# Moving the loads of a rotary-embedding kernel from a casting GpSimd DMA queue to float32 loads on SyncE's hardware queue, with ScalarE doing the cast and smaller buffer pools

## Chip, cores, metric

One core of one Trainium2 chip. The metric is the time of one execution on the device, in microseconds. All runs quoted here are fast (a single core, granted clock 1.0). "Span" is what the profiler shows from the first to the last instruction; a measured time is about 2 us longer than the span of the same run. The experiments ran in three later sessions, on chips that the record numbers 5, 3 and 12; the kernel before was measured again in each (medians 322.81, 323.12 and 323.17 us), and the ratios are taken within a session. Where two changed kernels of different sessions are subtracted below, that shift of up to 0.5 us is in the difference.

## The reference

```python
x: (8, 2048, 16, 64) float32      cos, sin: (2048, 32) float32
x1, x2 = x[..., :32], x[..., 32:]
out1 = x1 * cos - x2 * sin        # cos, sin broadcast over batch and heads
out2 = x1 * sin + x2 * cos
return concatenate([out1, out2], -1)          # float32, same shape as x
```

x and the output are 67.1 MB each. The arithmetic is slight, so this kernel mostly moves data: 16 tiles, each with a 4 MiB float32 read and a 4 MiB float32 write in HBM.

## The kernel before

Everything that moves goes through GpSimd's DMA queue. A load casts float32 to float16 on the way in, and a store casts float16 to float32 on the way out. The code is shortened: views and broadcasts are left out, and `# ...` marks a cut.

```python
const_pool = tile_pool(name="rope_const", bufs=1)
io_pool  = tile_pool(name="rope_io", bufs=3)      # xt and ot, three of each
tmp_pool = tile_pool(name="rope_tmp", bufs=3)
# ... the tables, cast on the way in
nc.gpsimd.dma_start(out=cos_sb, in_=cos_src)
nc.gpsimd.dma_start(out=sin_sb, in_=sin_src)

for it in range(NT * B):                          # 16 tiles
    # ...
    xt = io_pool.tile([P, J, H, D], f16)
    nc.gpsimd.dma_start(out=xt, in_=x[...])       # float32 -> float16
    ot = io_pool.tile([P, J, H, D], f16)
    # ... v1, v2
    nc.vector.tensor_mul(out=ot, in0=xt, in1=cos)  # 128x8192
    nc.vector.tensor_mul(out=v1, in0=x2, in1=sin)  # 128x4096, as the next three
    nc.vector.tensor_mul(out=v2, in0=x1, in1=sin)
    nc.vector.tensor_sub(out=o1, in0=o1, in1=v1)
    nc.vector.tensor_add(out=o2, in0=o2, in1=v2)
    nc.gpsimd.dma_start(out=out[...], in_=ot)     # float16 -> float32
```

The scheduler orders GpSimd's queue as four loads, four stores, four loads, and so on. The queue is one line: a store that is issued behind a load runs after it (the packet times below show one that stood 13.6 us).

## Time and profile before

| | before |
|---|---|
| measured | 322.81 us (median of 3; 322.52 to 323.58) |
| span | 321.2 us |
| VectorE busy | 210.7 us, 66% |
| DMA busy | 9 tenths or more in 38 of 40 slices |
| HBM read + written | 134.7 MB, 419 GB/s over the span |

From the page of the kernel before: the span, and the rows that cut it into 40 equal slices (busy tenths; GB/s that the DMA engines moved), then the HBM total.

```profile
span 321.2 us, 191 instructions
...
DVE  0089999970009999994004999999100799999800
...
DMA  6999999999999999999999999999999999999994
GB/s 98 212 218 214 218 275 433 428 445 424 314 226 202 222 220 361 445 433 428 445 231 214 224 204 240 439 416 449 433 373 224 208 216 224 288 449 441 416 449 167
...
HBM read 67.63 MB, written 67.11 MB: 419 GB/s over the span
```

DMA is full from start to end, and VectorE (DVE) idles for whole slices. The GB/s row alternates between about 215 (loads) and about 435 (stores), and that is not a difference in speed. The profile counts the bytes that land, and a casting load lands half of what it reads, so loads read about 430 GB/s as well. One 4 MiB transfer of either kind takes 4.19 MB / 432 GB/s = 9.7 us, and 32 of them take 310 us.

The issues part of the same page (line, operation, count, KB each, median us from issue to landing):

```profile
out_dram<-ot POOLq DMA_DIRECT2D x16, 4096.0 KB, 20.4
xt<-in_x_dram POOLq DMA_DIRECT2D x16, 2048.0 KB, 24.5
cos_sb<-in_cos_dram POOLq DMA_DIRECT2D x1, 128.0 KB, 3.2
sin_sb<-in_sin_dram POOLq DMA_DIRECT2D x1, 128.0 KB, 3.3
```

The tables lead the queue and land 3.3 us after issue. The timeline of GpSimd's queue near the end (start us, us, instruction, idle before and who ended it):

```profile
260.39 0.54 POOL L44 DMA_DIRECT2D xt<-in_x_dram  x1 [32.02 <-DVE v L66]
264.79 0.54 POOL L72 DMA_DIRECT2D out_dram<-ot  x1 [3.87 <-DVE ot L70]
277.94 0.54 POOL L72 DMA_DIRECT2D out_dram<-ot  x1 [12.61 <-DVE ot L70]
291.08 0.53 POOL L72 DMA_DIRECT2D out_dram<-ot  x1 [12.61 <-DVE ot L70]
304.22 0.53 POOL L72 DMA_DIRECT2D out_dram<-ot  x1 [12.61 <-DVE ot L70]
```

VectorE makes a tile every 13.1 us, but a store takes only 9.7 us. In spite of that the DMA row stays at 9. The packet records say why: the last four stores began to move at 278.4, 288.2, 297.9 and 307.6 us. The first of them was issued at 264.79 and stood 13.6 us behind loads in the same queue. That backlog (stores issued that still wait for the DMA engines) shrinks by about 3.4 us per store (13.1 less 9.7) and lasts just to the end.

### The profile page before, as it was taken

The page shows a single profiled execution, that of the slowest core. Times are in us where ns is not written, and L with a number is a line of the kernel's source. Part 1 is how long each engine was busy: PE and PEld are TensorE (multiplying, and loading weights), DVE is VectorE, ACT ScalarE, POOL GpSimd, SP SyncE. Part 2 cuts the span into 40 slices and gives each one's busy share as a digit, 9 for nine tenths or more (in the row PEclk, how much of TensorE's full clock was granted, in tenths as well). Part 3 has the DMA queues.
Part 4 walks back from the last instruction along what each step waited for, and adds up shares of the span by engine and source line. Part 5 has one row for each costly group of instructions (what it writes and reads, how often), then busy time and mean ns, then how long its engine had stood idle before and what let it go on. Part 6 is the DMA issues. An engine that isn't in the chain of part 4 may idle for free.

```text
span 321.2 us, 191 instructions
## 1 busy us (share of the span) xinstructions
DVE 210.7 (66%) x80; POOL 18.9 (6%) x38
## 2 busy tenths in 40 slices
DVE  0089999970009999994004999999100799999800
POOL 4001000010000100002000000000200000000000
DMA  6999999999999999999999999999999999999994
GB/s 98 212 218 214 218 275 433 428 445 424 314 226 202 222 220 361 445 433 428 445 231 214 224 204 240 439 416 449 433 373 224 208 216 224 288 449 441 416 449 167
DMA packets 5153, 100.94 MB, mean 314 GB/s; under 512 B 544, under 2 KB 1056, under 8 KB 1056
## 3 DMA queue, kind: packets, MB, share of 16 engines
q0 software_dynamic: 5152, 100.93, 100.0%
q14 instruction: 1, 0.01, 0.0%
HBM read 67.63 MB, written 67.11 MB: 419 GB/s over the span
## 4 chain that ended last, share of the span: by engine, by line
DVE 46%; DMA 27%; issue 20%; POOL 2%; POOLq 0%; DVEq 0%; PEldq 0%
DMA xt<-in_x_dram 27%; DVE ot L59 16%; DVE v L66 8%; DVE v L65 8%; DVE ot L70 8%; DVE ot L69 5%; POOL out_dram L72 1%; POOL cos_sb L37 0%; POOL sin_sb L38 0%; POOLq L101 0%; POOL xt L44 0%; POOLq L72 0%; DVEq L59 0%; PEldq L101 0%; POOLq L44 0%
## 5 line engine op out<-in xcount | busy, mean ns | idle before, releaser
L59 DVE TENSOR_TENSOR ot<-xt,cos_sb 128x8192 f16<-128x8192 f16 x16 | 70.7, 4421 | 93.2 <-DMA xt<-in_x_dram 93.1
L70 DVE TENSOR_TENSOR ot<-ot,v 128x4096 f16<-128x4096 f16 x16 | 36.6, 2285 | 0.0
L65 DVE TENSOR_TENSOR v<-xt,sin_sb 128x4096 f16<-128x4096 f16 x16 | 36.6, 2285 | 0.0
L69 DVE TENSOR_TENSOR ot<-ot,v 128x4096 f16<-128x4096 f16 x16 | 36.6, 2285 | 0.0
L66 DVE TENSOR_TENSOR v<-xt,sin_sb 128x4096 f16<-128x4096 f16 x16 | 36.6, 2285 | 0.0
L72 POOL DMA_DIRECT2D out_dram<-ot x16 | 8.6, 535 | 166.9 <-DVE ot L70 166.9
L44 POOL DMA_DIRECT2D xt<-in_x_dram x16 | 8.6, 550 | 117.9 <-DVE v L66 117.9
L37 POOL DMA_DIRECT2D cos_sb<-in_cos_dram x1 | 0.8, 825 | 0.8 <-PEq L101 0.8
L38 POOL DMA_DIRECT2D sin_sb<-in_sin_dram x1 | 0.7, 733 | 0.0
L90 POOL MEMSET const-float32-0.0<- 128x1 f32 x1 | 0.1, 98 | 0.2 <-issue 0.2
L90 POOL MEMSET const-bfloat16-1.0<- 128x1 bf16 x1 | 0.1, 101 | 0.0
L90 POOL MEMSET const-float32-1.0<- 128x1 f32 x1 | 0.1, 98 | 0.0
L90 POOL MEMSET const-uint8-127<- 128x1 uint8 x1 | 0.1, 98 | 0.0
## 6 DMA issues: line engine op xcount, KB each, us to landing
out_dram<-ot POOLq DMA_DIRECT2D x16, 4096.0 KB, 20.4
xt<-in_x_dram POOLq DMA_DIRECT2D x16, 2048.0 KB, 24.5
cos_sb<-in_cos_dram POOLq DMA_DIRECT2D x1, 128.0 KB, 3.2
sin_sb<-in_sin_dram POOLq DMA_DIRECT2D x1, 128.0 KB, 3.3
```

The lines of the kernel that those rows point to most:

```text
L37: nc.gpsimd.dma_start(out=cos_sb, in_=cos_src)
L38: nc.gpsimd.dma_start(out=sin_sb, in_=sin_src)
L44: nc.gpsimd.dma_start(out=xt, in_=x[b, s0 : s0 + T2].rearrange("(p j) h d -> p (j h d)", j=J),)
L59: nc.vector.tensor_mul(out=ot.rearrange("p j h (e d) -> p j (h e) d", d=Dh), in0=xt.rearrange("p j h (e d) -> p j (h e) d", d=Dh), in1=cos ...
L65: nc.vector.tensor_mul(out=v1, in0=x2, in1=sin_bb)
L66: nc.vector.tensor_mul(out=v2, in0=x1, in1=sin_bb)
L69: nc.vector.tensor_sub(out=o1, in0=o1, in1=v1)
L70: nc.vector.tensor_add(out=o2, in0=o2, in1=v2)
L72: nc.gpsimd.dma_start(out=out[b, s0 : s0 + T2].rearrange("(p j) h d -> p (j h d)", j=J), in_=ot,)
L90: nc = _bacc.Bacc("TRN2", target_bir_lowering=False, num_devices=1)
```

## The change

The intent is to let loads run on a queue of their own, so that they no longer wait in GpSimd's order behind stores, and to spare GpSimd their issue. The load now lands as float32, and ScalarE, idle until now, casts in SBUF. A float32 load buffer is twice as large, and the other pools are cut: three load buffers, two float16 buffers, two output buffers (before: three), one set of temporaries (before: three).

```diff
-    io_pool = ctx.enter_context(tc.tile_pool(name="rope_io", bufs=3))
-    tmp_pool = ctx.enter_context(tc.tile_pool(name="rope_tmp", bufs=3))
+    in_pool = ctx.enter_context(tc.tile_pool(name="rope_in", bufs=3))
+    half_pool = ctx.enter_context(tc.tile_pool(name="rope_half", bufs=2))
+    out_pool = ctx.enter_context(tc.tile_pool(name="rope_out", bufs=2))
+    tmp_pool = ctx.enter_context(tc.tile_pool(name="rope_tmp", bufs=1))
 ... (cos and sin: still two casting loads on GpSimd's queue)
-        xt = io_pool.tile([P, J, H, D], f16)
-        nc.gpsimd.dma_start(
-            out=xt,
+        xf = in_pool.tile([P, J * H * D], f32)
+        nc.sync.dma_start(
+            out=xf,
             in_=x[b, s0 : s0 + T2].rearrange("(p j) h d -> p (j h d)", j=J),
         )
+        xt = half_pool.tile([P, J, H, D], f16)
+        nc.scalar.copy(out=xt.rearrange("p j h d -> p (j h d)"), in_=xf)
 
-        ot = io_pool.tile([P, J, H, D], f16)
+        ot = out_pool.tile([P, J, H, D], f16)
```

More of the change, by code (lines that the diff above doesn't have):

```diff
@@ L20 @@
     f16 = mybir.dt.float16
+    f32 = mybir.dt.float32
     B, S, H, D = x.shape
@@ L29 @@
     const_pool = ctx.enter_context(tc.tile_pool(name="rope_const", bufs=1))
-    io_pool = ctx.enter_context(tc.tile_pool(name="rope_io", bufs=3))
-    tmp_pool = ctx.enter_context(tc.tile_pool(name="rope_tmp", bufs=3))
-    cos_src = cos.rearrange("(t p j) d -> p t (j d)", p=P, j=J)
-    sin_src = sin.rearrange("(t p j) d -> p t (j d)", p=P, j=J)
+    in_pool = ctx.enter_context(tc.tile_pool(name="rope_in", bufs=3))
+    half_pool = ctx.enter_context(tc.tile_pool(name="rope_half", bufs=2))
+    out_pool = ctx.enter_context(tc.tile_pool(name="rope_out", bufs=2))
+    tmp_pool = ctx.enter_context(tc.tile_pool(name="rope_tmp", bufs=1))
     cos_sb = const_pool.tile([P, NT, J * Dh], f16)
     sin_sb = const_pool.tile([P, NT, J * Dh], f16)
-    nc.gpsimd.dma_start(out=cos_sb, in_=cos_src)
-    nc.gpsimd.dma_start(out=sin_sb, in_=sin_src)
+    nc.gpsimd.dma_start(out=cos_sb, in_=cos.rearrange("(t p j) d -> p t (j d)", p=P, j=J))
+    nc.gpsimd.dma_start(out=sin_sb, in_=sin.rearrange("(t p j) d -> p t (j d)", p=P, j=J))
     for it in range(NT * B):
```

## The prediction

> **What bounds the kernel now.** DMA. The row of forty slices shows the DMA engines at 9 in every slice but the first and last, while VectorE is 66% busy and idles for whole slices. HBM read plus written is 134.7 MB, 419 GB/s over the 321.2 us span. In slices that hold only stores the page shows 428 to 449 GB/s. In slices that hold only loads it shows 202 to 226, but it counts the float16 that lands; the float32 read is twice that, about 430. So a 4 MiB transfer, load or store, costs about 4.19 MB / 432 GB/s = 9.7 us, and the cast makes a load no cheaper. Thirty-two of them are 310 us; about 11 us is start and end. The Trainium skill ("DMA: Bandwidth & Descriptors", Where 436 GB/s comes from) names a ceiling of 435 GB/s; the trace agrees to within its slices. The long waits in the waits view (VectorE for xt, 93.1 us; the store issue for VectorE, 166.9 us) are slack: the single queue always has work behind them, down to the last store.
>
> **What the change removes.** The blocking of loads behind stores in GpSimd's program order (groups of four loads, then four stores; the load issue waited 117.9 us for VectorE), and the loads' GpSimd issue time, 16 x 0.55 us, off the path. SBUF traffic of a load doubles (4 MiB land instead of 2), HBM traffic stays. The same skill page (Issuing engines are not separate DMA queues) says that all queues run on the same 16 engines, so I expect no more bandwidth: loads again about 9.7 us alone, about 19.4 us while a store shares the engines.
>
> **What it adds.** Sixteen ScalarE copies of 128x8192. The skill ("ScalarE: Activation LUTs", What ACT_TABLE_LOAD costs) gives 186 ns + 0.833 ns per element: an estimate of 7.0 us each, 112 us in all, overlapped with DMA except at the start and end. VectorE work per tile stays 4.42 + 4 x 2.29 = 13.4 us of records (13.1 us apart), 210 us in all.
>
> **What reaches the critical path.** Start: the first load leaves on SyncE's own queue rather than after cos and sin, saving about 2 us; but cos and sin now share the engines with 4 MiB loads and may land late (estimate 9 to 45 us), delaying VectorE. Loads prefetch meanwhile, so DMA stays busy. Middle: VectorE needs 13.1 us per tile against 19.4 us of DMA, so DMA still sets the pace. End: before, all last loads were done at about 280 us and a backlog of stores kept DMA full. After, loads and stores share, so the last load lands near 275 to 295 us, followed by copy 7.0, VectorE 13.1, store issue latency about 2.5, store 9.7: about 32 us, in which DMA has only about two other stores (20 us), or VectorE's 13.1 us per tile paces the remaining stores of 9.7. I estimate 8 to 14 us of idle DMA there.
>
> Sum: 3 start + 310 + 11 idle + 1.6 end + 1.6 (measured time minus profiled span, from before) = about 327.5 us.
>
> **What would show it.** ScalarE copy near 7.0 us x16. Average DMA rate in the middle near 430 GB/s, with loads and stores mixed. DMA below 9 tenths in some of the last five slices. VectorE total unchanged near 211 us. SyncE load waits on ScalarE.
>
> **What would make it wrong.** Hardware-queue float32 loads slower than 430 GB/s (at 409 it is about 335 us); small load packets starved by store packets, or the reverse; late sin delaying VectorE enough to empty the DMA queue early; or a backlog of stores long enough to hide the end (about 318 us).
>
> I expect 327.5 us, range 319 to 337; faster by over 2% 0.05, within 2% 0.53, slower by over 2% 0.42.

## The result

The changed kernel took 331.82 us (median of 4; 331.79 to 331.92), beside 322.66 us for the kernel before in the same rounds (median of 4). The ratio is 1.028, with a 95% interval of 1.0264 to 1.0296: slower by 2.8%. A ratio here is the mean time of one kernel's fast runs over the mean of the other's fast runs of the same rounds, so it is not quite the ratio of the medians.

The page of the changed kernel, the same rows:

```profile
span 330.1 us, 233 instructions
...
DVE  0005059999194884929578392955929398999940
...
DMA  8999997989999999999999999999999999975967
GB/s 320 420 419 436 403 447 318 441 385 445 445 445 441 385 445 445 445 421 405 445 445 445 409 417 445 445 442 413 417 445 441 445 389 441 381 318 246 389 254 318
...
HBM read 67.63 MB, written 67.11 MB: 408 GB/s over the span
```

HBM traffic is the same to the digit. In the middle the DMA row is full. There are dents at about one sixth of the span and in the last five slices. The groups of instructions and the issues, same columns as before (a group's line: count, busy us, mean ns, idle before and its releaser):

```profile
L50 ACT CAST xt<-xf 128x8192 f16<-128x8192 f32 x16 | 112.3, 7018 | 179.1 <-DVE v L68 164.8
L61 DVE TENSOR_TENSOR ot<-xt,cos_sb 128x8192 f16<-128x8192 f16 x16 | 70.8, 4423 | 91.1 <-DMA out_dram<-ot 65.3
L67 DVE TENSOR_TENSOR v<-xt,sin_sb 128x4096 f16<-128x4096 f16 x16 | 36.5, 2283 | 14.4 <-DMA sin_sb<-in_sin_dram 14.4
...
xf<-in_x_dram SPq DMA_DIRECT2D x16, 4096.0 KB, 36.0
out_dram<-ot POOLq DMA_DIRECT2D x16, 4096.0 KB, 27.4
cos_sb<-in_cos_dram POOLq DMA_DIRECT2D x1, 128.0 KB, 24.5
sin_sb<-in_sin_dram POOLq DMA_DIRECT2D x1, 128.0 KB, 42.6
```

VectorE's new waits are for an output buffer that a store has not yet emptied (65.3 us in all), and once for sin (14.4 us). sin now lands 42.6 us after issue instead of 3.3.

The dents, looked at closely: stretches of time (us from the span's start), their length, busy us and instructions of each engine, PEclk (TensorE's granted clock, which nothing here uses), share of DMA busy, GB/s. The engines stand in the order VectorE, ScalarE, GpSimd.

```profile
53.30:55.30 2.00, 2.00 (x2) 2.00 (x1) 0.57 (x1) 1.00 0.61 262
109.00:245.00 136.00, 92.57 (x35) 49.13 (x7) 3.74 (x7) 1.00 1.08 432
...
289.20:292.30 3.10, 3.10 (x2) 3.10 (x1) 0.53 (x1) 1.00 0.40 169
292.40:302.20 9.80, 9.80 (x5) 1.02 (x1) 0.00 (x0) 1.00 0.89 374
302.30:305.50 3.20, 3.20 (x2) 0.00 (x0) 0.53 (x1) 1.00 0.38 164
305.60:315.30 9.70, 9.70 (x5) 0.00 (x0) 0.00 (x0) 1.00 0.90 378
315.40:318.70 3.30, 1.62 (x1) 0.00 (x0) 0.53 (x1) 1.00 0.37 159
```

This view spreads a transfer's bytes over neighbouring stretches, so it shows a dent rather than a zero. The packet records are sharper: no packet at all moves from 53.2 to 55.3, 289.1 to 292.4, 302.3 to 305.6 and 315.4 to 318.7 us. Those are one gap of 2.1 us and three of 3.3 us, 12.0 us in all. VectorE is busy in all of them except half of the last.

And GpSimd's queue near the end, in the changed kernel:

```profile
276.27 0.53 POOL L74 DMA_DIRECT2D out_dram<-ot  x1 [18.87 <-DVE ot L72]
291.02 0.53 POOL L74 DMA_DIRECT2D out_dram<-ot  x1 [14.22 <-DVE ot L72]
304.17 0.53 POOL L74 DMA_DIRECT2D out_dram<-ot  x1 [12.61 <-DVE ot L72]
317.31 0.53 POOL L74 DMA_DIRECT2D out_dram<-ot  x1 [12.61 <-DVE ot L72]
```

The last three stores are issued 13.1 us apart, as before. But now their packets begin 1.4 us after each issue (292.4, 305.6, 318.7): there is no backlog, and the DMA engines wait for VectorE after every store.

The account, by the packet records (fast profiled runs):

| us | before | after |
|---|---|---|
| first packet of the kernel | 3.7 | 2.0 |
| time in which any DMA engine moved data | 315.9 | 314.5 |
| gaps with no packet at all | 0.0 | 12.0 |
| last packet to end of span (taken equal, see below) | 1.6 | 1.6 |
| span | 321.2 | 330.1 |

Start and transfer work are each a little better, by 1.6 (unrounded) and 1.4 us, and the gaps cost 12.0. (The records have a clock of their own. It is tied to the span here by taking the end as 1.6 us after the last packet; in both kernels the first load's last packet then ends within 0.1 us of the instruction that waited for it. The second row counts a moment as busy when at least one of the 16 engines moves data, so engines that wait for one another do not show as gaps.)

### The profile page after: what moved, and what is told of

It reads as the page before. It is cut to its first block, busy times and chain, and to the rows that moved or that the text cites. A ratio compares the mean times of both kernels' runs of the same rounds, so it can differ in the third digit from the quotient of the medians.

```text
span 330.1 us, 233 instructions
## 1 busy us (share of the span) xinstructions
DVE 211.5 (64%) x80; ACT 113.6 (34%) x17; POOL 10.3 (3%) x22
## 4 chain that ended last, share of the span: by engine, by line
issue 59%; DMA 22%; DVE 13%; POOL 2%; POOLq 0%; PEldq 0%
DMA sin_sb<-in_sin_dram 13%; DMA out_dram<-ot 9%; DVE ot L61 4%; DVE ot L71 3%; DVE v L68 3%; DVE v L67 2%; DVE ot L72 2%; POOL out_dram L74 2%; POOL cos_sb L38 0%; POOLq L103 0%; POOLq L74 0%; PEldq L103 0%
## 5 line engine op out<-in xcount | busy, mean ns | idle before, releaser
L50 ACT CAST xt<-xf 128x8192 f16<-128x8192 f32 x16 | 112.3, 7018 | 179.1 <-DVE v L68 164.8
L61 DVE TENSOR_TENSOR ot<-xt,cos_sb 128x8192 f16<-128x8192 f16 x16 | 70.8, 4423 | 91.1 <-DMA out_dram<-ot 65.3
L67 DVE TENSOR_TENSOR v<-xt,sin_sb 128x4096 f16<-128x4096 f16 x16 | 36.5, 2283 | 14.4 <-DMA sin_sb<-in_sin_dram 14.4
L50 ACT ACT_TABLE_LOAD x1 | 1.3, 1283 | 0.7 <-PEq L92 0.7
## 6 DMA issues: line engine op xcount, KB each, us to landing
sin_sb<-in_sin_dram POOLq DMA_DIRECT2D x1, 128.0 KB, 42.6
```

The lines of the kernel that those rows point to most:

```text
L50: nc.scalar.copy(out=xt.rearrange("p j h d -> p (j h d)"), in_=xf)
L61: nc.vector.tensor_mul(out=ot.rearrange("p j h (e d) -> p j (h e) d", d=Dh), in0=xt.rearrange("p j h (e d) -> p j (h e) d", d=Dh), in1=cos ...
L67: nc.vector.tensor_mul(out=v1, in0=x2, in1=sin_bb)
```

## The experiments

Theory A: the DMA engines do the same work at the same rate. The loss is their idle time: at the end, where VectorE paces the last stores and there is no backlog, and early, where the tables are late. That the small output pool decides the backlog was not yet part of it: for the second run A expected that a third output buffer would not help. This came with theory A1, after that run missed. Rival B: float32 loads on the hardware queue, landing twice the bytes and hopping through ScalarE, cost more per tile. Every run was correct except one. In the notes below, "n load / m output" counts float32 load buffers and output buffers; the changed kernel has 3 / 2.

### Tables ahead of x on SyncE's queue (3 / 2)

```diff
-    nc.gpsimd.dma_start(out=cos_sb, in_=cos...)
-    nc.gpsimd.dma_start(out=sin_sb, in_=sin...)
+    cos_f = const_pool.tile([P, NT, J * Dh], f32)
+    sin_f = const_pool.tile([P, NT, J * Dh], f32)
+    nc.sync.dma_start(out=cos_f, in_=cos...)
+    nc.sync.dma_start(out=sin_f, in_=sin...)
+    nc.scalar.copy(out=cos_sb, in_=cos_f)
+    nc.scalar.copy(out=sin_sb, in_=sin_f)
```

> As after, but cos and sin come in float32 on SyncE's queue ahead of the first x load and ScalarE casts them. Theory A (same DMA work; the added time is 12.0 us of idle DMA: 2.1 us early because sin lands at 44.7 us, and 3 x 3.3 us in the tail where VectorE paces the last stores): sin is there before 10 us, the early gap goes, the lead of loads over stores shrinks by about two tiles so one of the three tail gaps goes too; estimate 325.6 us (324 to 327.5). Rival B (a float32 load on the hardware queue, with its doubled landing and its ScalarE hop, costs about 0.55 us more per tile throughout): only the first microseconds change, 329 to 332 us.

Measured: 328.65 us, ratio to before 1.019 (1.017 to 1.021). The early gap and one of the three tail gaps went, as A said; two of 3.3 us stayed. But it missed A's 325.6 by 3 us and lies between the two forecasts, so by itself it settles little. Two things were not in the estimate. The first copy of x began at 16.9 us instead of 13.2. And the 16 DMA engines ran up to 5.4 us apart: the completion records of one load in mid kernel began between 143.1 and 148.5 us, against 0.2 us apart in the changed kernel. The time in which any DMA engine moved data rose from 314.5 to 316.7 us, so "the same work" of A does not hold here. Why the engines drifted, and whether the drift is what made it longer, is open.

### Two load buffers, three output buffers (2 / 3)

```diff
-    in_pool = ctx.enter_context(tc.tile_pool(name="rope_in", bufs=3))
+    in_pool = ctx.enter_context(tc.tile_pool(name="rope_in", bufs=2))
-    out_pool = ctx.enter_context(tc.tile_pool(name="rope_out", bufs=2))
+    out_pool = ctx.enter_context(tc.tile_pool(name="rope_out", bufs=3))
```

> As after, but two float32 load buffers and three output buffers (same SBUF within 16 KiB a partition). Theory A: cos and sin still come late, all buffers fill before the first store, so the tail stays paced by VectorE: estimate 330.9 us (329 to 332.5), sin still near 43 to 45 us. Rival B: unchanged, 331 to 332 us. This run separates little by itself; it is one corner of a square with e1 and e3.

Measured: 323.19 us, ratio 1.002 (1.000 to 1.004). A clear miss, 7.7 us better than expected. It was meant as a corner of a square and became the best hint. sin landed 22.2 us after issue instead of 42.6. With two load buffers the third load can only leave when the first copy is done, SyncE's queue runs dry for a moment, and the tables slip through: by the packet records 284 of the 512 table packets went between 22 and 24 us, after 20 to 33 in every 2 us before that. Which of the two pools brought the rest is asked below.

### Both edits (2 / 3, tables first)

> Both edits: cos and sin first on SyncE's queue, two load buffers, three output buffers. Theory A: stores start by 37 us, VectorE runs up to three tiles ahead of the stores, a backlog of stores covers the tail, no idle DMA over 1 us after the first load: estimate 318.2 us (316.5 to 320.5), faster than both kernels, although the hardware queue, the float32 landing and the ScalarE copies all stay. Rival B: those three are the cost, so 328 to 332 us.

Measured: 326.47 us, ratio 1.013 (1.010 to 1.015). Another miss, 8.3 us worse than A's number, 1.5 us below the rival's range. Of the gaps with no packet only one of 2.8 us was left. But the last load came late: its copy began at 291.1 us, against 286.4 in the changed kernel, where that copy waited for a float16 buffer although its load had landed at 279.4. The time in which any DMA engine moved data was 318.0 us, 3.5 us more than in the changed kernel and 3.1 more than with the same buffers and the tables on GpSimd's queue (314.9): that is more of the 8.3 us that A missed than the one gap is. The completion spread between engines in mid kernel was 5.8 us here; that it is the cause is not shown. With only two load buffers the last load is not ahead of the rest, and copy, VectorE and store (33 us from 291.1 to the span's end at 324.4) follow it in the open.

### A lighter VectorE in the last four tiles (wrong result on purpose, 3 / 2)

```diff
+        light = it >= NT * B - 4
-        nc.vector.tensor_mul(out=v2, in0=x1, in1=sin_bb)
+        if not light:
+            nc.vector.tensor_mul(out=v2, in0=x1, in1=sin_bb)
-        nc.vector.tensor_add(out=o2, in0=o2, in1=v2)
+        if not light:
+            nc.vector.tensor_add(out=o2, in0=o2, in1=v2)
```

> Wrong result on purpose: as after, but in the last four tiles VectorE leaves out two of its five operations (second sine product and the addition), 8.7 us per tile instead of 13.1; nothing else changes, sin stays late. Theory A: in the tail VectorE is then quicker than a store (9.7 us), the three gaps of 3.3 us go or shrink under 1 us each: estimate 321.2 us (319.5 to 324). Rival B: VectorE is only 64% busy and DMA is the limit, so a lighter VectorE in the last four tiles saves at most the shorter last tile, 4.4 us: 327 to 332 us.

Measured: 321.43 us, ratio to before 0.997 (0.994 to 0.999): A's 321.2 within 0.2 us, and outside the rival's range. Removing 16.8 us of VectorE's busy time (211.5 to 194.7) from the last four tiles took 10.4 us off the time of the changed kernel. The three tail gaps are gone, the early one (1.9 us) is still there. The end of GpSimd's queue:

```profile
271.95 0.53 POOL L78 DMA_DIRECT2D out_dram<-ot  x1 [14.60 <-DVE ot L74]
286.70 0.53 POOL L78 DMA_DIRECT2D out_dram<-ot  x1 [14.22 <-DVE ot L74]
296.21 0.53 POOL L78 DMA_DIRECT2D out_dram<-ot  x1 [8.98 <-DVE ot L74]
305.89 0.53 POOL L78 DMA_DIRECT2D out_dram<-ot  x1 [9.14 <-DVE ot L74]
```

The last three stores now leave 9.5 and 9.7 us apart, at the pace of the DMA engines. So an engine that is busy 64% of the span sets the pace in the last 50 us.

### A third output buffer, nothing else (3 / 3)

```diff
-    out_pool = ctx.enter_context(tc.tile_pool(name="rope_out", bufs=2))
+    out_pool = ctx.enter_context(tc.tile_pool(name="rope_out", bufs=3))
```

> As after, with a third output buffer and nothing else: sin still lands near 44 us, the 2 us early gap stays. Theory A1 (the tail is paced by VectorE because two output buffers let at most two stores queue up; a third lets VectorE run one more tile ahead while loads and stores share, so the tail has a backlog): the three tail gaps shrink to at most one, 321 to 324 us. Theory A2 (late tables alone made the loads run ahead, and the output buffers do not matter; in the earlier run with three output and two load buffers it was the load buffers that helped): 330 to 332 us.

Measured: 321.30 us (5 runs, 321.27 to 321.41), ratio 0.994 (0.993 to 0.996). One number in the source took 10.5 us off the changed kernel (331.82 to 321.30), with the late sin, the hardware queue, the float32 landing and the 16 ScalarE copies all in place. With all its costs in place rival B would leave the time near 331 us, so it is falsified as the cause of the loss. The other pools that the diff cuts, float16 buffers and temporaries, were not varied; with three output buffers no gap at the end is left for them to explain. The page's DVE and DMA rows show only the early dent left:

```profile
DVE  0005049999999692975929569294792938899920
...
DMA  8999996999999999999999999999999999999996
```

The stretches of this run, columns as before, show the same early dent, the same 432 GB/s in the middle, and a full end:

```profile
53.30:55.30 2.00, 2.00 (x2) 2.00 (x1) 0.57 (x1) 1.00 0.61 262
109.00:245.00 136.00, 92.54 (x35) 49.12 (x7) 3.73 (x7) 1.00 1.08 432
...
289.00:318.00 29.00, 17.05 (x7) 0.00 (x0) 1.07 (x2) 1.00 0.99 416
```

The start times of the last four stores' packets, beside the changed kernel and the kernel before, show the mechanism:

| first packet of store (us) | 13th | 14th | 15th | 16th |
|---|---|---|---|---|
| before | 278.4 | 288.2 | 297.9 | 307.6 |
| changed kernel (3 / 2) | 278.7 | 292.4 | 305.6 | 318.7 |
| third output buffer (3 / 3) | 278.6 | 288.3 | 298.0 | 307.7 |

By the packet records the last load's data ended at 273.4 us in the changed kernel and at 273.3 here: loads are not the difference. With three output buffers VectorE is one tile further on when the loads end, so one more store stands in line, and that covers three times 3.4 us.

### Two load buffers, nothing else (2 / 2)

> As after, with two load buffers instead of three and nothing else: the third load can only leave after the first copy, so cos and sin get through near 24 us as they did in the run with both changes; two output buffers stay. Theory A1: early gap gone, two tail gaps of about 3 us, late completion of the last load: 327 us (325 to 329.5). Theory A2: as fast as the run with both changes, 322 to 324.5 us.

Measured: 327.80 us, ratio 1.014 (1.013 to 1.016), as A1 said. Together with 323.19 for 2 / 3 this isolates the output buffer again: a third one is worth 4.6 us with two load buffers and 10.5 us with three. The load buffers matter too, in either direction: going from three to two gained 4.0 us with two output buffers (331.82 to 327.80) and lost 1.9 us with three (321.30 to 323.19).

### Tables in two halves, in order of need (3 / 2)

```diff
-    nc.gpsimd.dma_start(out=cos_sb, in_=cos...)       # all 16 tiles' tables
-    nc.gpsimd.dma_start(out=sin_sb, in_=sin...)
+    for t in range(NT):                               # two halves
+        nc.gpsimd.dma_start(out=cos_sbs[t], in_=cos_src[:, t, :])
+        nc.gpsimd.dma_start(out=sin_sbs[t], in_=sin_src[:, t, :])
```

> As after, but cos and sin are each loaded in two halves in order of need (cos and sin of the first eight tiles, then of the last eight), on the same queue, same bytes. If the tables are late because their 512 byte packets on the GpSimd queue alternate one by one with the 32 KiB load packets (1.21 us each), then half as many packets must pass before the first sin is in: cos near 14 us, sin near 25 us instead of 44.7; first store near 38 us; early gap gone; total 326.5 us (324.5 to 328.5), near the run with the tables first. If the tables are late for a reason that does not count packets, sin stays near 43 us and the total at 330 to 332 us.

Measured: 329.78 us, ratio 1.021 (1.019 to 1.022). The first sin was in at 26.1 us, by the chain of work that ended last (start us, us, what), first of the changed kernel:

```profile
2.08 42.58 DMA sin_sb<-in_sin_dram
```

then of this run:

```profile
1.91 24.15 DMA sin_sb<-in_sin_dram
```

Half the packets, a little over half the wait: landing follows the number of table packets. The Trainium skill ("DMA: Bandwidth & Descriptors", Queues, rings and completion order) says that each DMA engine takes turns between the queues it has work for, a packet at a time. This trace agrees in number, if its packet records are what the page calls packets (the page counts several descriptors to a packet, which the records do not show): from 6.4 to 43.5 us about as many x packets began, 476, as table packets, 512. Each table is 16 packets of 512 bytes per engine, and between cos (25.84 us, when the first VectorE operation could start) and sin (44.66 us) lie 18.8 us, or 16 turns of 1.18 us, where one 32 KiB x packet takes 1.23 us. In the changed kernel 512 table packets were spread over 37 us, 20 to 33 in most stretches of 2 us, where 16 engines that pass one between any two x packets would pass 26. The early gap went, worth 2.1 us; the time fell by 2.0. But the total missed its range (324.5 to 328.5): all three tail gaps stayed. So having sin at 26 us instead of 45 was worth 2 us and left the end of the kernel as it was. That late tables also make the loads run too far ahead is not borne out by this run. It is not ruled out for tables that come earlier still: with the tables first, cast by 4.8 us, one gap at the end did go.

### Halved tables and a third output buffer (3 / 3)

> As after, with a third output buffer and the tables loaded in two halves in order of need. If the two costs add (three tail gaps, about 10 us, from the two output buffers; one early gap of 2 us from the late tables), both go: no idle DMA over 1 us between the first load and the last store, 321.3 minus 2.0 = 319.3 us (318.3 to 320.5), faster than the kernel before by about 1.1%. If they do not add (tables in time let the loads run less far ahead, and a tail gap returns), 320.5 to 324 us.

Measured: 319.36 us (6 runs, 319.28 to 319.71) against 323.17 (11 runs), ratio 0.989 (0.987 to 0.992). The two costs add: 331.82 - 10.5 - 2.0 = 319.3. No gap without a packet is left. The span is 3.7 us shorter than that of the kernel before: 1.6 us from the start (first packet at 2.1 us) and 2.1 us from the time in which any DMA engine moved data (315.9 to 313.8 us); why the second fell is open. Its span and DMA row:

```profile
span 317.5 us, 237 instructions
...
DMA  8999999999999999999999999999999999999996
```

This is the fastest kernel, 1.1% under the kernel before, a difference clear of noise but under 2%.

### Last tile cut in two (2 / 3)

> A try for a kernel faster than both: two load buffers, three output buffers, and the last tile alone cut in two halves (two loads, copies, sets of operations and stores of 2 MiB). The last chain (copy, five operations, store issue, store) shrinks from about 32 us to about 17 us, so the one gap of 2.8 us in the tail goes; DMA work is unchanged. Estimate 320.3 us (319 to 322). If the last load's late completion (its last data ended at 280.5 us, its copy began at 287.9) moves later with it, no gain: 322.5 to 324 us.

Measured: 320.47 us, ratio 0.992 (0.990 to 0.993), as estimated. It keeps the third output buffer and has only two load buffers; beside the 323.19 us of the same buffers with a whole last tile, the shorter last chain is worth 2.7 us, and no gap without a packet is left.

### Control: the kernel before with its tables on SyncE's queue

```diff
-    nc.gpsimd.dma_start(out=cos_sb, in_=cos_src)
-    nc.gpsimd.dma_start(out=sin_sb, in_=sin_src)
+    nc.sync.dma_start(out=cos_f, in_=cos_src)         # float32 tiles
+    nc.sync.dma_start(out=sin_f, in_=sin_src)
+    nc.scalar.copy(out=cos_sb, in_=cos_f)
+    nc.scalar.copy(out=sin_sb, in_=sin_f)
```

> A control on the kernel before: one GpSimd queue with casting loads stays, but cos and sin come in float32 on SyncE's queue, cast by ScalarE, so that the first x load leaves first on the GpSimd queue. If the start of the kernel before (its first packet at 3.7 us, the tables ahead of x) is all that a second queue can save it, 320.9 us (320 to 322); if the start hides behind something else, 322.5 to 323.2 us.

Measured: 322.07 us (6 runs, 320.52 to 322.53), ratio 0.997 (0.994 to 0.999). It lies a hair above its first range. The first packet moved at 2.6 us instead of 3.7. A better start alone gains about 0.3%, so it is a small part of what the best kernel gains.

## Why the prediction was right

The time fell within the range (319 to 337), 4.3 us above the point forecast, and the likeliest class, within 2%, had 0.53 against 0.42 for the one that came. Point by point:

- **DMA bounds both kernels, and a second queue brings no bandwidth: right.** From 14 to 23 us the engines run float32 loads of the hardware queue and a few table packets, at 433 GB/s; in the middle, loads and stores mixed run at 432. The kernel before moved about 430 of either kind. The skill's ceiling of 435 GB/s ("DMA: Bandwidth & Descriptors", Where 436 GB/s comes from) fits these rates. The same passage says that about 358 GB/s binds for transfers between HBM and SBUF; the 432 here, with one core at work, lies above that.
- **ScalarE copies of 7.0 us, hidden: right.** 7018 ns measured, and the third-buffer run shows that they cost nothing. The skill's formula gives an estimate of 186 + 0.833 x 8192 = 7010 ns ("ScalarE: Activation LUTs", What ACT_TABLE_LOAD costs).
- **Start about 2 us earlier: right,** 1.6 us. **Tables landing 9 to 45 us late: right,** at the far end, 44.7 us. That "DMA stays busy" meanwhile failed by a gap of 2.1 us, which the prediction had listed among its risks.
- **Idle DMA at the end, 8 to 14 us: right,** 9.9 us, with the second of the two mechanisms it offered: VectorE's 13.1 us per tile paces stores of 9.7. The first, a chain of 32 us behind the last load, is not what happened here; the last load had landed (its completion was signalled) at 279.4 us and its copy waited for a buffer until 286.4. The only arithmetic that the prediction gave, 32 us less two stores (20 us) = 12 us, belongs to that first mechanism, so that the number fits is in part luck. In the two runs with two load buffers and three output buffers and whole last tiles that chain did end the kernel.
- **The mis-sized term** is the DMA work in "3 start + 310 + 11 idle + 1.6 end + 1.6". Measured: 2.0 + 314.5 + 12.0 + 1.6 + 1.8 = 331.9. The prediction had itself seen that before "about 11 us is start and end", but carried only 4.6 of it over (3 start, 1.6 end). By the packet records the kernel before already had 315.9 us in which some DMA engine moved data, 5.5 us more than 32 times 9.7. Taking over that measured figure would have put the forecast within 2 us, and on the other side of 2%.
- **What the prediction did not name** is the cause behind the empty tail: the diff's pools, two output buffers where there were three. It was read as "a backlog of stores long enough to hide the end (about 318 us)" among the risks, without asking which number in the diff decides it. One more buffer gives 321.3, and with tables in time 319.4.

## What to carry to other kernels

When a change pays for a new stage with buffers, look at the buffers that it takes from the last stage. In this kernel, which DMA bounds, the output buffers held the backlog that keeps DMA full when the loads have ended; without it VectorE, slower per tile (13.1 us) than a store (9.7) though only 64% busy, set the pace there. Look also at a small transfer that everything waits for, when large ones run on another queue: loading the tables in halves, in order of need, gained 2.0 us. Putting them whole ahead of x is no sure remedy: it gained 3.2 us with three load and two output buffers (331.82 to 328.65) and lost 3.3 us with two and three (323.19 to 326.47).

## What the Trainium skill lacked or had wrong

- "DMA: Bandwidth & Descriptors" says that engines take turns between queues packet by packet, but not what this does to a small transfer. Here 128 KB of sin took 3.3 us when alone in front and 42.6 us beside a queue of 32 KiB packets.
- The same page says a completion write lands only after every earlier write of that DMA engine, across its queues, and gives no size for it. Beside a stream of stores the completion records of SyncE's loads lasted 1.25 us in mid kernel, and 2.5 to 7.3 us for the last load, in steps of about 1.21 us, about one store packet (1.23 us) each. With two load and three output buffers the last data ended at 280.5 us and the copy began at 287.9. The skill's sentence fits; the length is not on the page.
- The same page describes packets as preferably up to 4096 bytes; nearly all bytes of the changed kernel moved in packets recorded as 32 KiB, on both queues. Whether such a record is what the page calls a packet, no run here shows.
- I found no page that tells that the order of the first transfers can set the DMA engines drifting: 0.2 us apart in the changed kernel, 2.4 us with two load buffers and three output buffers, 5.4 us with the tables first on the hardware queue. The cause is open.
- "ScalarE: Activation LUTs" was right on the copy (7010 ns against 7018) and on the table load (1283 ns on both).
